# One layer of a hybrid streaming encoder on one core: x and the first part of w_ada arrive laid out by feature block, and the first three projection blocks begin with 704 of 1056 tokens

## The chip, the core and the metric

The kernel runs on one core of a Trainium2 chip. A core has five engines, each with its own in-order list of instructions: PE (TensorE, matrix products into PSUM), ACT (ScalarE), DVE (VectorE), POOL (GpSimd) and SP (SyncE, which here only starts transfers). Sixteen DMA engines move data between HBM and the on-chip memory SBUF. An engine waits at an instruction until the semaphores that it names have been raised, and everything behind that instruction on the same engine waits with it.

The metric is the device time of one execution in microseconds (us). Three executions of the kernel before took 1600.66, 1601.08 and 1601.70 us, so the median is 1601.08 us.

## The reference

T = 1056 tokens (1024 of a prompt and 32 of a sample) of D = 1024 features go through one layer. What matters here is its beginning:

```python
mod = jax.nn.silu(c) @ w_ada + b_ada
sh1, sc1, gt1, sh2, sc2, gt2 = jnp.split(mod[:, None, :], 6, axis=-1)

h = rmsnorm(x, g_mix) * (1 + sc1) + sh1
u = h @ w_in
qa, ka, va, qm, km, vm, om, ip, fp, ga, gm = jnp.split(u, _split_points(), axis=-1)
```

Prompt and sample have a condition c of their own, so sh1 and sc1 are two vectors of 1024 each. rmsnorm(x, g) is x * rsqrt(mean(x*x) + 1e-6) * g. Attention over qa, ka, va, an mLSTM, two projections, a second norm and an FFN follow. The first inputs of the layer are w_ada[:, 0:2048] (8 MB, for sh1 and sc1), x (4.3 MB) and the columns of w_in.

## The kernel before

Features lie on the 128 partitions: x, h and all later activations are held as eight feature blocks of 128 x 1056 (KD = 8). The tokens are cut into three tiles of 352 (TILES). A projection block is 128 columns of w_in. For accuracy each float32 operand is split in two fp32r parts, a high one (rounded) and a low one (the rest), and a product is three passes (PASSES): high by high, low weight by high h, high weight by low h. One tile of one block is therefore 8 feature blocks x 3 passes = 24 products of 128x128 by 128x352.

The order on PE, ACT, DVE and POOL is the order in which the code is written; no scheduler changes it. SP's transfers go in the order written as far as buffers are free. The front of the program, up to the first blocks of attention, runs as follows.

- **x.** Eight transfers bring x token by token (L220). DVE sums the squares of each token (square_sum, L273), PE turns the 64 pieces of 128x128 with transposes (L281), and ACT copies them out of PSUM (L282). POOL makes the reciprocal roots (L299, a power of -0.5), and PE and ACT spread them over the partitions as RB (bcast_cols, L242 and L245).
- **w_ada.** Eight transfers of 1 MB bring its rows (L264). For each, PE forms the part of sc1 (first_ada, L322: eight float32 matmuls, two instructions each in the trace) and DVE the part of sh1 (shift_part, L314). The sum for sh1 over the partitions is taken by PE at the end (row_sums, L348 and L352). Since every element of sh1 and sc1 needs all rows of w_ada, no block of h is ready before the last transfer.
- **h.** For feature block j, scaled_x (L375, DVE) multiplies x by scale and RB, high_h (L386, ACT) adds the shift and rounds, low_h (L392, DVE) forms the low part.
- **First products.** first_units(L475) runs the K and V blocks of head pair 0 together, feature block by feature block, over all three token tiles: 144 products. K is accumulated in three banks of the pool mm (three buffers), V in psS and psT. In the last feature block K's products come first, so that ACT takes K out (L553, L556) while PE does V's.
- **Then** unit() (L443) runs the Q block, 72 products, with buffers of mm, and V's transposes (L612) stand between them. The block behind it, K of head pair 1, is the first of the regular run that fills the rest of the front part of the layer. Weights of a block are split by ACT (L409) and DVE or POOL (L410) into four buffers of the pool wsp; the next two halves wait there for the buffers of the block that is done.

x by features is also written to HBM (xres, L1508) and read back for the residual add (L1552). The pool tmp has four buffers of 128 x 1056 float32. The last feature block of the first products is ordered by this line, which the prediction's last wait turns on:

```python
            if k == KD - 1:
                order.sort(key=lambda x: (x[0], x[2]))
```

Of the kernel before, what the change touches and what calls it, by code (L numbers as in the profile page):

```python
# [17 lines left out]
P = 128  # L18
# [121 lines left out]
def hybrid_stream_step(  # L140
    ctx: ExitStack,
    tc: tile.TileContext,
    x_prompt, x_sample, cache_k, cache_v, state_conv, state_C, state_n, state_m,
# [9 lines left out]
    xp, xs_in = x_prompt[0], x_sample[0]  # L153
    w_in, w_ada, w_out, w_down = w_in[0], w_ada[0], w_out[0], w_down[0]
# [53 lines left out]
    ssq = cp.tile([P, NB], F32, name="ssq")  # L208
    pool.memset(ssq, 1.0)
# [4 lines left out]
    xtok = []  # L214

    for i in range(KD):
        if i % 2 == 0:
            xt = slot([P, 2, D])
            xtok += [xt[:, 0], xt[:, 1]]
        sp.dma_start(xtok[i], xp[i * P:(i + 1) * P])  # L220
    pool.dma_start(cols, params)
    xsm = tmpt((TS, D))
    sp.dma_start(xsm, xs_in)


    csil = cp.tile([P, KD, 2], F32, name="csil")

    def param_cols():
        act.activation(csil, cols[:, R_C:R_C + 16].rearrange("p (c k) -> p k c", c=2), AF.Silu)
# [19 lines left out]
    rstd = cp.tile([P, NB], F32, name="rstd")  # L249
    xres = dr.tile([KD, P, T], F32, name="xres")  # L250
    xTs, xTp, xns = [], [], []
    for j in range(KD):
        if j % 2 == 0:
            xT2 = slot([P, 2, T])
            xTp.append(xT2)
        xTs.append(xT2[:, j % 2])

    was = []
    first_ws, first_cols = [], (KA, VA)

    def load_ada(n):
        while len(was) < n:
            wa = slot([P, 2048])
            sp.dma_start(wa, w_ada[len(was) * P:(len(was) + 1) * P, 0:2048])  # L264
            was.append(wa)

    load_ada(KD)

    def square_sum(i):
        n = P if i < 8 else TS  # L270
        src = xtok[i] if i < 8 else xsm
        junk = tmpt((P, D), BF16)
        dve.tensor_tensor_reduce(junk[:n], src, src, 1.0, 0.0, ALU.mult, ALU.add, ssq[:n, i:i + 1])  # L273

    def x_transposes(g, j):

        pt = mmt()
        for n in range(2):
            for i in range(2):
                at = (2 * n + i) * P  # L280
                pe.transpose(pt[:, at:at + P], xtok[2 * g + i][:, (j + n) * P:(j + n + 1) * P], ident)  # L281
        act.activation(xTp[j // 2][:, :, g * 256:(g + 1) * 256], pt.rearrange("p (n t) -> p n t", n=2), AF.Copy)  # L282

    for g in range(4):
        for i in range(2):
            square_sum(2 * g + i)
# [1995 lines left out]
```

## Time and profile before

| What | Value |
|---|---|
| median of three executions | 1601.08 us |
| the profiled execution, its own time | 1600.87 us |
| its span in the trace | 1598.5 us |
| granted PE clock in that execution | 0.998 |
| DVE busy in the span | 70% |
| ACT busy in the span | 50% |
| POOL busy in the span | 26% |
| last of the eight blocks of x (L281 goes on) | 14.45 us |
| last of the eight blocks of w_ada (L322 goes on) | 36.22 us |

All times in the trace count from the start of the span; the execution's own time is 2.4 us longer than the span. A row of the timeline gives start, length, engine, source line, instruction, what it writes and reads, the number of instructions merged into it, and in brackets how long the engine had been idle before it and what it had waited for. A row of the groups gives the line, the shape, the count, then busy us and mean ns of one instruction, then the idle time before them.

### The profile page before, as it was taken

Reading aid. Unit: us, or ns where it says so; the run is one execution under the profiler, and the core shown is the slowest. Engines: PE = TensorE matmul, PEld = TensorE weight load, DVE = VectorE, ACT = ScalarE, POOL = GpSimd, SP = SyncE. Lnnn points to the kernel's source line nnn. Section 1 sums busy time; section 2 is a strip of 40 time slices with the busy share of each in tenths; the row PEclk is TensorE's granted clock in tenths of the full one; section 3 lists DMA queues with packets and bytes.
Section 4 is the critical chain, followed back from the end, with each engine's and each line's share of the span. In section 5 each row is a group of like instructions: output and inputs, shape, how many; then the busy total and the mean of one; then the engine's idle time right before and its main releaser. Section 6 shows DMA issues by size and latency. Waiting matters only on the chain.

```text
span 1598.5 us, 27336 instructions
## 1 busy us (share of the span) xinstructions
PE 1569.2 (98%) x10197; PEld 1549.3 (97%) x10197; DVE 1122.9 (70%) x2285; ACT 791.3 (50%) x1749; POOL 423.3 (26%) x450
## 2 busy tenths in 40 slices
PE   7999999999999999999999999999999999999997
PEld 6999999999999999999999999999999999999997
DVE  7766555556766845546655699898898986799754
ACT  3665463544555545444434655544445444544443
POOL 1343242433223311000012100675565650000001
PEclk9999999999999999999999999999999999999999
DMA  9823223343132332775453311223222237427454
GB/s 362 268 81 97 94 83 108 91 137 109 36 97 65 87 86 87 127 257 174 130 152 113 96 55 59 89 67 105 70 88 86 68 94 240 136 80 251 137 153 127
DMA packets 209906, 193.48 MB, mean 121 GB/s; under 512 B 11483, under 2 KB 179071, under 8 KB 208751
## 3 DMA queue, kind: packets, MB, share of 16 engines
q1 hardware_dynamic: 207214, 189.92, 38.7%
q10 hardware_dynamic: 2528, 1.77, 0.4%
q8 instruction: 80, 1.31, 0.4%
q14 instruction: 52, 0.42, 0.1%
q0 software_dynamic: 32, 0.06, 0.0%
HBM read 153.24 MB, written 41.63 MB: 122 GB/s over the span
## 4 chain that ended last, share of the span: by engine, by line
PE 91%; DVE 3%; DMA 2%; ACT 2%; issue 1%; SPq 0%; POOL 0%; ACTq 0%; DVEq 0%; POOLq 0%
PE mm L443 41%; PE psb L1811 18%; PE mm L1811 10%; PE mm L2214 3%; PE mm L878 3%; PE psb L2214 2%; PE psV L783 2%; PE psb L2057 2%; PE psS L725 2%; DMA s<-in_w_ada_dram 1%; PE psT L752 1%; PE mm L2057 1%; DMA t<-in_x_sample_dram 1%; PE psV L1112 1%; PE mm L475 1%
## 5 line engine op out<-in xcount | busy, mean ns | idle before, releaser
L443 PE MATMUL mm<-s,wsp 128*128 128x352 f32 x4104 | 687.0, 324 | 0.1
L443 PEld LDWEIGHTS mm<-s,wsp 128*128 128x128 f32 x4104 | 657.3, 188 | 1.8 <-issue 0.4
L410 DVE TENSOR_TENSOR wsp<-wraw,wsp 128x512 fp32r<-128x512 f32 (+1 forms) x280 | 235.6, 858 | 127.4 <-ACT wsp L409 125.3
L1811 PE MATMUL psb<-s,wsp 128*128 128x352 f32 x1611 | 271.7, 322 | 1.6 <-DVE wsp L410 0.9
L409 ACT ACTIVATE wsp<-wraw 128x512 fp32r<-128x512 f32 x336 | 199.5, 617 | 139.0 <-PE psb L1811 42.4
L1811 PEld LDWEIGHTS psb<-s,wsp 128*128 128x128 f32 x1611 | 260.5, 188 | 2.1 <-DVE wsp L410 1.1
L1811 PE MATMUL mm<-s,wsp 128*128 128x352 f32 x933 | 159.3, 322 | 0.0
L1811 PEld LDWEIGHTS mm<-s,wsp 128*128 128x128 f32 x933 | 151.2, 188 | 0.5 <-DVE wsp L410 0.5
L745 POOL TENSOR_SCALAR st<-st,mx 128x640 f32<-128x640 f32 (+5 forms) x72 | 53.1, 738 | 186.3 <-DVE mx L744 168.3
L1207 DVE CUSTOM_DVE_ANT_0 junk<-wa,t 128x512 bf16<-128x512 f32 x128 | 94.9, 742 | 2.8 <-DMA wa<-in_w_mod_dram 1.8
L410 POOL TENSOR_TENSOR wsp<-wraw,wsp 128x512 fp32r<-128x512 f32 x56 | 74.1, 1343 | 58.2 <-ACT wsp L409 56.8
L739 DVE CUSTOM_DVE_ANT_0 st<-psS,bias 128x640 f32<-128x640 f32 (+5 forms) x72 | 44.5, 618 | 57.1 <-PE psS L725 41.9
L740 ACT ACTIVATE st<-st,mx 128x640 f32<-128x640 f32 (+5 forms) x72 | 47.9, 666 | 63.2 <-DVE mx L739 62.1
L1758 POOL TENSOR_TENSOR t<-t,sl 128x352 f32<-128x352 f32 x19 | 18.4, 968 | 213.1 <-ACT sl L1756 213.1
L759 ACT ACTIVATE pT<-psT 128x640 fp32r<-128x640 f32 (+3 forms) x80 | 38.7, 493 | 62.6 <-PE psT L752 47.5
L2126 POOL TENSOR_TENSOR fst<-fst 128x1 f32<-128x1 f32 (+1 forms) x6 | 1.2, 192 | 236.7 <-ACT t L2119 236.7
L764 DVE TENSOR_TENSOR pT<-psT,pT 128x640 fp32r<-128x640 f32 (+3 forms) x80 | 44.0, 558 | 22.2 <-ACT pT L759 22.2
L1420 POOL TENSOR_TENSOR wraw<-wraw,raw 128x512 f32<-128x512 f32 x33 | 55.8, 1704 | 0.9
L878 PE MATMUL mm<-s,s 128*128 128x264 f32 (+3 forms) x432 | 54.5, 283 | 0.0
L2214 PE MATMUL mm<-s,wsp 128*128 128x352 f32 x330 | 54.4, 324 | 0.0
L2214 PEld LDWEIGHTS mm<-s,wsp 128*128 128x128 f32 x330 | 53.0, 188 | 0.0
L878 PEld LDWEIGHTS mm<-s,s 128*128 128x128 f32 (+1 forms) x432 | 52.0, 179 | 0.5
(369 smaller groups left out, 2482.2 us busy)
## 6 DMA issues: line engine op xcount, KB each, us to landing
wraw<-in_w_in_dram SPq DMA_DIRECT2D x38, 512.0 KB, 4.0
wraw<-in_w_gate_up_dram SPq DMA_DIRECT2D x33, 512.0 KB, 3.9
wa<-in_w_mod_dram SPq DMA_DIRECT2D x64, 256.0 KB, 2.8
wraw<-in_w_down_dram SPq DMA_DIRECT2D x32, 512.0 KB, 4.1
a_d<-t SPq DMA_DIRECT2D x22, 528.0 KB, 2.7
g_d<-t SPq DMA_DIRECT2D x16, 528.0 KB, 3.7
x<-xres SPq DMA_DIRECT2D x16, 528.0 KB, 8.6
t<-g_d SPq DMA_DIRECT2D x16, 528.0 KB, 4.5
```

The source lines that it names most:

```text
L409: act.activation(dst[:, 0], src, AF.Copy)
L410: eng.tensor_tensor(dst[:, 1], src, f(dst[:, 0]), op=ALU.subtract)
L443: pe.matmul(pt[:, :hi - lo], wt[(w0 + k) // 4][:, a, (w0 + k) % 4], xt[k][:, b, lo:hi], start=(k == 0 and q == 0), stop=(k == n - 1 and q ...
L739: dve.tensor_tensor_reduce(so, sv, bi, -1.0, 3.0e38, ALU.add, ALU.min, mx[:n, 1:2])
L740: act.activation(st[:n, :w], st[:n, :w], AF.Exp, bias=mx[:n, 1:2], scale=-1.0, accum_out=mx[:n, 2:3])
L745: pool.tensor_scalar(st[:n, :w], st[:n, :w], mx[:n, 3:4], 1.0, op0=ALU.mult, op1=ALU.mult)
L878: pe.matmul(pt[:n, :wd], hs[k][:, a, i * P:i * P + n], whl[b][:, k, :wd], start=(k == 0 and q == 0), stop=(k == KD - 1 and q == 2))
L1207: dve.tensor_tensor_reduce(junk, wa, crow[:, c], 1.0, 0.0, ALU.mult, ALU.add, at)
L1420: self.eng.tensor_tensor(a(dst), a(x), a(y), op=op)
L1811: pe.matmul(acc, wt[:, a, k], x[k][:, b], start=(start and not onto and k == 0 and q == 0), stop=(stop and k == 3 and q == 2), skip_group_ ...
L2057: pe.matmul(acc, wt[k // 4][:, u, k % 4], piece_of[k, i][:, v], start=(k == 0 and q == 0), stop=(k == KP - 1 and q == 2))
L2214: pe.matmul(acc, wt[(k - k0) // 4][:, u, (k - k0) % 4], piece_of[k, 2][:, v], start=(k == 0 and q == 0), stop=(k == NF - 1 and q == 2))
```

## The change

**Inputs.** x comes transposed from the host, one array of eight feature blocks (128 x 1056). The first 2048 columns of w_ada come as two sets of eight tiles of 128 x 1024, one tile for each feature block of sc1 ("scale") and one for each of sh1 ("shift"), so that one tile of 512 KB holds all that a feature block of the output needs. The shift tiles of blocks 0 to 2 are stored with the input features on the partitions, like the scale tiles; those of blocks 3 to 7 with the output features on the partitions.

**Order of the transfers.** First tokens 0 to 703 of the eight blocks of x (CUT = 704, eight transfers of 352 KB), then w_ada's tiles of block 0, the first halves of the K, V and Q weights, w_ada's tiles of block 1, the last 352 tokens of x, w_ada's tiles of block 2, the second weight halves, and the tiles of blocks 3 to 7. The small array of parameters (cols) is started by ACT instead of POOL.

**Conditioning.** PE and ACT make a copy of silu(c) on all partitions (crow), by 16 transposes and four activations. sc1 of a block is eight float32 matmuls with two moving columns (scale_sums, L324). sh1 of blocks 0 to 2 is made in the same way, and of blocks 3 to 7 by DVE, one reduction for each condition (shift_sums, L331).

**Squares.** ACT squares x (L296), DVE adds two blocks at a time (L299), PE sums over the partitions with a column of ones (token_sums, L309). This is done for the 704 early tokens first, and for the 352 late ones in rounds 1 and 2 of the products.

**Rounds.** first_units now runs K, V and Q of head pair 0 on the two early token tiles: in round k the 18 products of feature block k stand in three groups of six (one for each pass), with the scale sums of block k+1 between the first and the second group, and in rounds 1, 2 and 3 the sums of the late squares, and the spreading of the late roots, between the second and the third. Behind the eight rounds come 48 products of K and V on the late tile; Q's late tile is left to unit(). h is made in place: scaled_x multiplies x by RB (DVE), high_h and whole_h (both ACT, with scale and shift) give the rounded and the whole h, and low_h (DVE) the difference.

The x transposes, square_sum, first_ada, row_sums, and the first write of x to xres are gone; the residual add reads x from the input.

The diff, cut to its core:

```diff
-    for i in range(KD):
...
-        sp.dma_start(xtok[i], xp[i * P:(i + 1) * P])
-    pool.dma_start(cols, params)
+    act.dma_start(cols, params)
...
+    CUT = TILES[2][0]
     for j in range(KD):
...
+        sp.dma_start(xTs[j][:, :CUT], x_t[j][:, :CUT])
+
+    first_cols = (KA, VA, QA)
...
+    crow = slot([P, 2, D])
+    load_ada()
+    load_first(0)
+    load_ada()
+    for i, xp in enumerate(xTp):
+        sp.dma_start(xp[:, :, CUT:], x_t[2 * i:2 * i + 2].rearrange("n p t -> p n t")[:, :, CUT:])
+    load_ada()
+    load_first(1)
+    for _ in range(3, KD):
+        load_ada()
...
+    SHIFT_PE = 3
...
+    def conditioning():
...
+        for c in range(2):
+            for h in range(2):
+                pt = mmt()
+                for i in range(4):
+                    k = R_C + 8 * c + 4 * h + i
+                    pe.transpose(pt[:, i * P:(i + 1) * P], cols[:, k:k + 1].to_broadcast([P, P]), ident)
+                act.activation(crow[:, c, h * 512:(h + 1) * 512], pt, AF.Silu)
...
+    def square(j, lo, hi):
+        sq[j] = tmpt()
+        act.activation(sq[j][:, :hi - lo], xTs[j][:, lo:hi], AF.Square)
...
+    def token_sums(j, tiles, begin, end):
...
+                pe.matmul(tok[:b - a, col:col + 1], sq[j][:, a - a0:b - a0], ones[:, 0:1],
+                          start=(begin and col == 0), stop=end, skip_group_check=True)
...
+    def scale_sums(j, i=0):
+
+        at = 2 * (KD * i + j)
+        for k in range(KD):
+            pe.matmul(psH[:, at:at + 2], was[j][:, i, k * P:(k + 1) * P], csil[:, k], start=(k == 0), stop=(k == KD - 1),
+                      skip_group_check=True)
...
+    def shift_sums(j, c):
+        dve.tensor_tensor_reduce(junk, was[j][:, 1], crow[:, c], 1.0, 0.0, ALU.mult, ALU.add, sha[:, c, j:j + 1])
...
+    def scaled_x(j, lo, hi):
+        x = xTs[j][:, lo:hi]
+        dve.tensor_tensor(x, x, RB[:, lo:hi], op=ALU.mult)
...
+            act.activation(hs[j][:, 0, a:b], xTs[j][:, a:b], AF.Identity, scale=s1[:, c, j:j + 1],
+                           bias=sh1[:, c, j:j + 1])
+
+    def whole_h(j, lo, hi):
...
+            act.activation(x, x, AF.Identity, scale=s1[:, c, j:j + 1], bias=sh1[:, c, j:j + 1])
+
+    def low_h(j, lo, hi):
+        dve.tensor_tensor(hs[j][:, 1, lo:hi], xTs[j][:, lo:hi], f(hs[j][:, 0, lo:hi]), op=ALU.subtract)
...
+        pts = [[S[:, :512], S[:, 512:]], [psA[:, :512], mmt()], [mmt(), mmt()], ]
+        last = [tok, psH]
...
+        def late_squares(j0, j1):
+            for j in range(j0, j1):
+                square(j, *late)
+                if j > j0:
+                    add_squares(j0, j, NT)
+            token_sums(j0, [late], j0 == 0, j1 == KD)
...
+        for k in range(KD):
+            n = k + 1
+            for i in range(3):
+                for t in range(2):
+                    product(k, i, 0, t)
+            if n < KD:
+                scale_sums(n)
+                if n < SHIFT_PE:
+                    scale_sums(n, 1)
+                else:
+                    shift_sums(n, 0)
+                scaled_x(n, 0, CUT)
+                scale_done(n)
+                shift_done(n, 0)
+                high_h(n, 0, CUT)
+                whole_h(n, 0, CUT)
+            low_h(k, 0, CUT)
+            for i in range(3):
+                for t in range(2):
+                    product(k, i, 1, t)
             if k in (1, 2):
-                if k == 1:
-                    first_split(1)
+                late_squares(4 * k - 4, 4 * k)
+            if k == 3:
+                token_roots(2, 0)
...
+            if SHIFT_PE <= n < KD:
+                shift_sums(n, 1)
+                shift_done(n, 1)
+            late_h(k - 3)
+            for i in range(3):
+                for t in range(2):
+                    product(k, i, 2, t)
...
+        for k in range(KD - 3, KD + 2):
+            late_h(k)
+        for k in range(KD):
+            for q in range(3):
+                for i in range(2):
+                    product(k, i, q, 2)
...
+        W.advance()
...
-            yield lo, hi, done[t] if done else unit(w, 0, hs, lo, hi)
+            yield lo, hi, done[t] if done and t < len(done) else unit(w, 0, hs, lo, hi)
...
-    for j in range(KD):
-        sp.dma_start(xres[j], xTs[j])
-    first_units([run.w for run in segs[0][1][:2]])
+    first_units()
...
-        sp.dma_start(x2[j], xres[j])
+        sp.dma_start(x2[j], x_t[j])
```

Three places in the order of the instructions matter. The number behind a name is that of its buffer. First PE, where the products begin. Before, the last sums for sh1 stand ahead of the first products of K (mm_61, mm_62) and V (psS_60, psT_47) and between them; in the seven rounds behind this piece there are products alone:

```order
L352 MATMUL psV_46_266<-csil_107,s_17_128 128x64
L348 MATMUL psV_46_266<-ones_85,t_49_269 128x64
L352 MATMUL psV_46_266<-csil_107,s_17_128 128x64
L348 MATMUL psT_47_267<-ones_85,t_48_268 128x64
L475 MATMUL mm_61_426<-s_65_432,wsp_56_398 128x352
L475 MATMUL psS_60_425<-s_65_432,wsp_58_400 128x352
L348 MATMUL psT_47_267<-ones_85,t_48_268 128x64
L475 MATMUL mm_62_427<-s_65_432,wsp_56_398 128x352
L475 MATMUL psS_60_425<-s_65_432,wsp_58_400 128x352
L348 MATMUL psT_47_267<-ones_85,t_48_268 128x64
L475 MATMUL mm_63_428<-s_65_432,wsp_56_398 128x352
L475 MATMUL psT_47_267<-s_65_432,wsp_58_400 128x352
```

After, this is the middle of round 1 (h block s_45), from the last product of the first pass over the scale and shift sums of block 2 (16 float32 matmuls into psV), the second pass, and the sums of the late squares (t_47) to the first product of the third pass:

```order
L453 MATMUL mm_40_285<-s_45_325,s_44_294 128x352
L324 MATMUL psV_20_152<-csil_93,s_11_124 128x2 x16
L453 MATMUL psS_37_282<-s_45_325,wsp_33_261 128x352 x2
L453 MATMUL psT_19_151<-s_45_325,wsp_42_289 128x352
L453 MATMUL mm_38_283<-s_45_325,wsp_42_289 128x352
L453 MATMUL mm_39_284<-s_45_325,s_44_294 128x352
L453 MATMUL mm_40_285<-s_45_325,s_44_294 128x352
L309 MATMUL psT_19_151<-ones_85,t_47_376 128x1 x2
L309 MATMUL psT_19_151<-ones_85,t_47_376 96x1
L453 MATMUL psS_37_282<-s_45_325,wsp_33_261 128x352 x2
```

The small matmuls moved from ahead of the products into the rounds, and the third pass of round 1 now stands behind the late squares on PE.

Second, ACT in the same rounds. Before, one round on ACT is the rounding of one block of h and the 32 sample tokens apart (here two rounds):

```order
L386 ACTIVATE s_71_568<-s_70_545,sh1_270 128x1024
L385 ACTIVATE s_70_545<-s_70_545,sh1_270 128x32
L386 ACTIVATE s_71_568<-s_70_545 128x32
L386 ACTIVATE s_72_594<-s_70_545,sh1_270 128x1024
L385 ACTIVATE s_70_545<-s_70_545,sh1_270 128x32
L386 ACTIVATE s_72_594<-s_70_545 128x32
```

After, ACT takes sc1 and sh1 out of PSUM (s1, sh1), makes the high and the whole h of blocks 1 and 2 (s_45, s_46), and then squares the late tokens of blocks 0 to 3 (t_47 to t_50):

```order
L328 ACTIVATE s1_150<-psV_20_152,gb1_147,cols_91 128x2
L337 ACTIVATE sh1_149<-psV_20_152,cols_91 128x2
L351 ACTIVATE s_45_325<-s_1_95,sh1_149,s1_150 128x704
L357 ACTIVATE s_1_95<-s_1_95,sh1_149,s1_150 128x704
L328 ACTIVATE s1_150<-psV_20_152,gb1_147,cols_91 128x2
L337 ACTIVATE sh1_149<-psV_20_152,cols_91 128x2
L351 ACTIVATE s_46_366<-s_2_96,sh1_149,s1_150 128x704
L357 ACTIVATE s_2_96<-s_2_96,sh1_149,s1_150 128x704
L296 ACTIVATE t_47_376<-s_1_95 128x352
L296 ACTIVATE t_48_378<-s_1_95 128x352
L296 ACTIVATE t_49_381<-s_2_96 128x352
L296 ACTIVATE t_50_384<-s_2_96 128x352
```

The squares for which PE's row t_47 waits come behind the whole h of block 2, and that behind the scale and shift sums of block 2 on PE.

Third, the end of the first products on ACT. Before, ACT takes the K block (mm_61 and on) out of PSUM and only then splits the next weights (wsp_82, wsp_83):

```order
L386 ACTIVATE s_79_658<-s_73_598 128x32
L553 ACTIVATE s_80_682<-mm_61_426 64x352 x2
L553 ACTIVATE s_80_682<-mm_62_427 64x352 x2
L556 ACTIVATE kf_81_683<-mm_62_427 128x192
L553 ACTIVATE s_80_682<-mm_63_428 64x352 x2
L556 ACTIVATE kf_81_683<-mm_63_428 128x352
L409 ACTIVATE wsp_82_698<-wraw_75_629 128x512
L409 ACTIVATE wsp_83_699<-wraw_75_629 128x512
L587 ACTIVATE t_85_708<-psS_60_425 128x352 x2
L587 ACTIVATE t_85_708<-psT_47_267 128x352
```

After, the split of the next weights (wsp_63, wsp_64, in the buffers of the K weights) stands ahead, and then K's tiles (psS_37, psT_19) and V's (psT_19, mm_38):

```order
L368 ACTIVATE wsp_63_724<-wraw_59_579 128x512
L368 ACTIVATE wsp_64_725<-wraw_59_579 128x512
L566 ACTIVATE s_66_732<-psS_37_282 64x352 x4
L569 ACTIVATE kf_67_733<-psS_37_282 128x192
L566 ACTIVATE s_66_732<-psT_19_151 64x352 x2
L569 ACTIVATE kf_67_733<-psT_19_151 128x352
L600 ACTIVATE t_68_750<-psT_19_151 128x352
L600 ACTIVATE t_68_750<-mm_38_283 128x352
L600 ACTIVATE t_68_750<-psV_20_152 128x352
L652 ACTIVATE t_71_759<-mm_39_284 128x352
```

On PE the last of the late products and the first of Q's late tile then stand thus; that tile's bank, mm_74, is the third buffer of mm again, which V's second tile (mm_38) holds until ACT has read it:

```order
L453 MATMUL psT_19_151<-s_62_603,wsp_34_262 128x352
L453 MATMUL psV_20_152<-s_62_603,wsp_43_290 128x352
L453 MATMUL psT_19_151<-s_62_603,wsp_34_262 128x352
L453 MATMUL psV_20_152<-s_62_603,wsp_43_290 128x352
L402 MATMUL mm_74_779<-s_41_287,s_44_294 128x352 x3
L402 MATMUL mm_74_779<-s_45_325,s_44_294 128x352 x3
```

The first product of Q's late tile moved behind ten instructions of ACT, the second of which, the split into wsp_64, waits for the last product that reads the K weights.

305 lines of the change are left out of this document (118 added, 187 removed).

## The prediction

> **What bounds the kernel now.** The page first, its busy times by engine:
>
> ```profile
> PE 1569.2 (98%) x10197; PEld 1549.3 (97%) x10197; DVE 1122.9 (70%) x2285; ACT 791.3 (50%) x1749; POOL 423.3 (26%) x450
> ```
>
> PE is the bound: a change of the front is worth what it moves the moment from which PE runs its regular blocks. Two rows of the timeline fix the front: the first product, and the first product of the block behind Q, K of head pair 1.
>
> ```profile
> 41.34 0.43 PE L475 MATMUL mm<-s,wsp 128*128 128x352 f32 x1 [0.65 <-ACT s L386]
> 81.52 5.94 PE L443 MATMUL mm<-s,wsp 128*128 128x352 f32 x36
> ```
>
> So PE reaches the regular run at about 81.4 us. How much of that is waiting? The busy times by stage, cut at the first data, the first product and that moment, and then PE's two longest waits up to there:
>
> ```profile
> 0.00:4.64 4.64, 0.00 (x0) 0.03 (x1) 0.00 (x0) 1.28 (x1) 1.63 (x10) 1.00 0.54 189
> 4.64:41.33 36.69, 30.63 (x231) 27.61 (x231) 30.79 (x41) 13.56 (x33) 2.52 (x2) 1.00 1.01 379
> 41.33:81.36 40.03, 39.31 (x247) 37.93 (x248) 31.15 (x46) 24.93 (x54) 14.28 (x17) 1.00 0.82 271
> ...
> PE mm L281 <- DMA s<-in_x_prompt_dram: 6.6, 3, 4.6
> PE psT L322 <- DMA s<-in_w_ada_dram: 3.0, 6, 0.7
> ```
>
> The first busy column is PE's, the last two numbers are the share of the DMA engines and GB/s. From 4.64 to 41.33 PE idles 6.1 us, mostly for transfers, and from there to 81.36 only 0.7. The front looks bound by DMA (share 1.01), and the chain of waits runs through w_ada; yet PE has 70 us of its own work in it. An earlier start helps only so far: waiting less can gain 7 us at most, unless PE's work shrinks.
>
> **The change part by part.** Does it shrink? Prices on PE: a stretch of 18 products, x's transposes, eight of L322's matmuls (two instructions each), and float32 matmuls with one moving column, which stand elsewhere in the program:
>
> ```profile
> 90.72 2.88 PE mm L443 x18
> ...
> 5.83 2.39 PE L281 MATMUL mm<-ident,s 128*128 128x128 f32 x10 [0.74 <-DMA s<-in_x_prompt_dram]
> ...
> 7.59 5.67 PE L281 MATMUL mm<-ident,s 128*128 128x128 f32 x40
> ...
> 17.26 2.05 PE L322 MATMUL psT<-csil,s 128*128 128x128 f32 x16
> ...
> 894.93 0.36 PE L1583 MATMUL psV<-ones,sl 128*128 128x1 f32 x2
> 895.15 0.36 PE L1581 MATMUL psV<-ones,t 128*128 128x1 f32 x2
> 895.38 0.36 PE L1583 MATMUL psV<-ones,sl 128*128 128x1 f32 x2
> 895.60 0.31 PE L1581 MATMUL psV<-ones,t 128*96 128x1 f32 x2
> 895.77 0.31 PE L1583 MATMUL psV<-ones,sl 128*96 128x1 f32 x2
> ```
>
> A product takes 2.88/18 = 0.16 us, a transpose 5.67/40 = 0.14. A float32 matmul with one moving column starts 0.225 us after the one before (two steps from 894.93 to 895.38), hardly less than L322's 2.05/8 = 0.256 with 128; with only 96 weight columns it is 0.17. Two-column matmuls are not in the trace, so I take 0.225, the nearest row, and keep 0.17 and 0.256 as ends. After, PE has 88 of them for scale and shift (3x16 + 5x8) and 30 for token sums, 26.6 us. They replace 64 of L322 (16.4), 22 row sums at about 0.225 (5.0) and 72 transposes of x (10). With crow's 16 transposes (2.3 to 3.8) the new work is 29 to 30 us against 31. PE's work does not shrink; what is left to win is the idle time.
>
> Prices of ACT, DVE and POOL, from the groups by shape (mean ns behind the busy time), and nine copies in a row:
>
> ```profile
> L1610 ACT ACTIVATE s<-x,amod 128x352 fp32r<-128x352 f32 x16 | 9.3, 588 | 7.9 <-DVE x L1609 7.9
> L1627 ACT ACTIVATE x<-x,amod 128x32 f32<-128x32 f32 x8 | 2.5, 311 | 0.0
> L1027 ACT ACTIVATE s<-t,cols 128x1024 f32<-128x1024 f32 x8 | 9.9, 1234 | 0.0
> L409 ACT ACTIVATE s<-x 128x352 fp32r<-128x352 f32 x68 | 29.4, 484 | 0.0
> L409 ACT ACTIVATE s<-s 128x1056 fp32r<-128x1056 f32 x4 | 4.3, 1082 | 2.2 <-DVE s L1241 2.2
> 9.32 4.53 ACT L282 ACTIVATE s<-mm 128x512 f32<-128x512 f32 x9 [0.26 <-PE mm L281]
> L1561 DVE TENSOR_TENSOR t<-t,t 128x352 f32<-128x352 f32 x24 | 12.6, 526 | 0.8
> L1241 DVE TENSOR_TENSOR s<-s,s 128x1056 f32<-128x1056 f32 x4 | 5.0, 1260 | 2.6 <-ACT s L1240 2.6
> L273 DVE CUSTOM_DVE_ANT_0 t<-s 128x1024 bf16<-128x1024 f32 x8 | 9.7, 1225 | 6.0 <-DMA s<-in_x_prompt_dram 5.8
> L1588 POOL TENSOR_TENSOR rs<-rs,mhalf 128x4 f32<-128x4 f32 x3 | 3.3, 1086 | 19.5 <-DVE rs L1586 19.5
> ```
>
> On the lines between these, 704 columns cost ACT 0.93 with scale and shift and 0.78 without (a square), and DVE 0.89; a tiny activation costs 0.28, a shift reduction 1.3 with its read-out, a power 1.1. Independent copies start about 0.1 before the one before has ended (nine of 0.6 in 4.53).
>
> *Up to the first product.* It needs crow's place on ACT, the squares of 704 tokens, and RB. The start of the timeline, and the transfer of cols:
>
> ```profile
> cols<-in_params_dram POOLq DMA_DIRECT2D x1, 62.0 KB, 5.9
> ...
> 0.82 3.89 SPq L220 DMA_DIRECT2D s<-in_x_prompt_dram  x8
> ...
> 6.76 0.60 ACT L282 ACTIVATE s<-mm 128x512 f32<-128x512 f32 x1 [4.67 <-PE mm L281]
> 7.62 0.60 ACT L282 ACTIVATE s<-mm 128x512 f32<-128x512 f32 x1 [0.26 <-PE mm L281]
> ...
> 25.00:30.00 5.00, 4.11 (x35) 3.73 (x34) 4.97 (x5) 0.00 (x0) 0.00 (x0) 1.00 1.02 423
> ```
>
> Cols took 5.9 us to land. Started by ACT among x's first transfers it should land with x's first block, which PE had at 4.64; I take 4.6, between 3.5 (it is only 62 KB) and 7.5 (as slow as before). Four transposes and a copy came every 0.86 us (6.76 to 7.62), so crow, four of these, is done at 8.8. ACT, in order, then squares eight blocks, 0.7 each back to back and half a us lost to the adds: 15.3. DVE's last add ends at 16.2, PE's last six sums at 17.6; then PE has 16 matmuls for block 0 (3.6 us, under which the two powers, 2.2, are hidden; were they not, they would cost that much), the transposes of the roots, and then come RB, s1 and sh1, and the high h: first product at 23.7 instead of 41.3. Data is there: at 0.42 MB per us the 4.7 MB of early x, block 0 and three weight halves land by about 16, all 14.3 MB by about 40, and w_ada's last tiles are wanted after 70. SP issues 34 transfers here instead of 21, at 0.49 us (3.89/8) half the time that they take to move. Gain **17.6**.
>
> *Behind it.* 216 products are 34.6 us in both. The small matmuls of blocks 1 to 7 (72) and of the late squares (6) now stand here, 17.6, and three transposes, 0.4; before, 11 row sums did, 2.5. V's nine transposes, 1.4, stand ahead of the moment 81.4 now and behind Q's last tile after, so that they come on top there. Loss 18.0 + 1.4 - (2.5 + 1.4) = **15.5**.
>
> *New waits.* Round 1: once PE has done the sums of block 2, ACT needs s1 and sh1 (0.6), the high and the whole h (1.85), four squares (1.6, and 0.4 waiting for an add), DVE the last add (0.5): with handovers 5.2, of which PE's second pass covers 1.0. The token sums, and behind them on PE the third pass, wait 4.2. Round 2 is the same with 1.4 for the adds, since two buffers of tmp are all that is left to the squares: 5.3. Round 3: the late roots cross DVE, POOL, PE and ACT, 1.4. Block 0's second tile, 0.9. Rounds 4 and 6 wait for DVE, which has two reductions and 704 and 352 columns twice, 5.2 a round back to back, against PE's 18 x 0.16 + 8 x 0.225 = 4.7: together 2.1. Last, Q's late tile waits for the bank of V's second tile. ACT's copies out of PSUM at this place now, K's and V's:
>
> ```profile
> 66.65 1.88 ACT L553 ACTIVATE s<-mm 64x352 fp32r<-64x352 f32 x4 [3.55 <-PE mm L475]
> 68.54 0.33 ACT L556 ACTIVATE kf<-mm 128x192 f32<-128x192 f32 x1
> 69.69 0.46 ACT L556 ACTIVATE kf<-mm 128x352 f32<-128x352 f32 x1
> 71.96 0.80 ACT L587 ACTIVATE t<-psS 128x352 f32<-128x352 f32 x2
> ```
>
> They run beside PE's products of V and Q. After, ACT starts the split into wsp_64 only when K's last product is done (0.6), then takes out six half tiles of K (6 x 0.47), kf (0.8) and two tiles of V (0.9), some 5.2 in all, with PE idle. Sum of the waits 19.1, against 81.4 - 41.3 - 34.6 - 2.5 - 1.4 = 1.6 now: loss **17.5**.
>
> Sum: 23.7 + 34.6 + 18.0 + 1.4 + 19.1 = 96.8 instead of 81.4, **15.4 us later**. What lies behind is PE's own work and moves as a whole. The first writes of x to xres gain nothing by their absence: ACT and POOL waited for them once, PE never.
>
> **Rivals.** (1) The late squares do not hold PE (adds and squares get done earlier than I reckon): 4.2 + 5.3 less, so +5.9 and 1606.8. For it speaks that ACT is only half busy; against it that each group crosses ACT, DVE and PE in a fixed order behind the sums of the next block.
>
> (2) PE's clock falls in the new gaps. After its first 4.6 us without work PE made ten transposes in 2.39 us, 0.24 each, and later forty at 0.14: 1.0 us lost. After three gaps over 4 us as much each is +3, 1619.3. The granted clock reads 1.00 throughout, so the trace leaves open whether the clock was the cause. [...]
>
> (3) The other side: behind the first product PE waits for nothing, because ACT and DVE keep ahead of it. Then 96.8 - 19.1 = 77.7, 3.7 earlier than 81.4: 1597.2. It decides as soon as the waits sum to less than 3.7; the last one alone is 5.2.
>
> (4) The change does not bring what it says: the early start is eaten exactly, 1600.9.
>
> **How the numbers follow.** The profiled execution took 1600.87 us, 0.2 under the median of 1601.08. 1600.9 + 15.4 = 1616.3; I say 1616. My forecast has a chance of 0.64, with its own ends from cols (-1.1 to +2.9), the small matmuls (118 at 0.17 to 0.256: -6.5 to +3.7, the low end only if two columns are far cheaper than one) and ACT's tiny instructions (1.5 either way): 1609 to 1622. Rival 1 has 0.14, rival 2 0.11, rival 3 0.05, rival 4 0.06. The range takes in rivals 1 and 2: 1606 to 1623. Faster by over 0.2% (3.2 us, about what a measurement of this kernel can tell from no change) has 0.05, the same 0.06, slower 0.89.
>
> **What would show it.** Right: a first product near 24 us, three idle times of PE of 4 to 5 us (before L309 in rounds 1 and 2, before the first L402), and K of head pair 1 near 95. Wrong: L324 under 0.17 us a matmul, or L309 without a wait, towards rivals 1 and 3; products at twice their time behind a gap would be rival 2. A gap of PE that comes from a transfer would upset the whole sum.

## The result, and the profile after

The changed kernel takes 1648.23 us (median of 4 runs, 1642.10 to 1649.23), the kernel before 1601.39 (4 runs): a ratio of 1.0282, 95% interval 1.0270 to 1.0294. It is slower, as forecast, but by 47 us instead of 15. The profiled span grew from 1598.5 to 1646.1, by 47.6.

The page of the changed kernel, its busy times by engine and PE's clock in 40 slices of 41 us:

```profile
PE 1600.2 (97%) x10205; PEld 1580.4 (96%) x10205; DVE 1108.3 (67%) x2287; ACT 813.1 (49%) x1786; POOL 416.0 (25%) x440
...
PEclk9689999999999999999999999999999999999999
```

PE executes 8 instructions more than before and is busy 31 us longer. That cannot be waiting; and slices two and three say that the clock was at 0.6 and 0.8. Before, all 40 digits are 9. The stages, cut at the first product and at the first product of the block behind Q (the columns are those of the prediction's windows):

```profile
0.00:30.49 30.49, 21.27 (x103) 20.58 (x103) 5.74 (x12) 12.12 (x21) 2.53 (x11) 1.00 0.98 346
30.49:123.67 93.18, 76.80 (x375) 73.85 (x376) 43.85 (x74) 47.89 (x100) 8.01 (x9) 0.74 0.36 123
```

The first product came 10.9 us earlier (41.34 to 30.49), forecast 17.6. From there to K of head pair 1 it took 93.2 us instead of 40.2 (81.52 - 41.34), 53.0 more, forecast 31.6. Behind that another 5.4 were lost (47.6 + 10.85 - 53.0), forecast 1.4. PE's longest waits up to there:

```profile
PE psT L309 <- DVE t L299: 11.4, 3, 5.1
PE mm L402 <- ACT t L600: 6.3, 1, 6.3
PE mm L288 <- DMA cols<-in_params_dram: 4.5, 1, 4.5
PE psS L453 <- ACT s L351: 2.1, 2, 1.7
```

The long waits are those of the forecast, at its places. Behind the first product the waits sum to 16.4 us (93.18 - 76.80), forecast 19.1. So the loss is in PE's *busy* time: 76.8 us where the forecast had 34.6 of products and 18.0 of small matmuls. The timeline of PE (start, length, line, operation, count, in brackets the idle time before) shows how:

```profile
11.20 9.52 PE L309 MATMUL psT<-ones,t 128*128 128x1 f32 x48 [3.06 <-DVE t L299]
20.58 6.97 PE L324 MATMUL psV<-csil,s 128*128 128x2 f32 x32
27.41 1.41 PE L227 MATMUL mm<-ident,roots 128*128 128x128 f32 x6
30.49 0.66 PE L453 MATMUL psS<-s,wsp 128*128 128x352 f32 x1 [1.66 <-ACT s L351]
...
40.63 0.49 PE L453 MATMUL psT<-s,wsp 128*128 128x352 f32 x1
40.92 0.49 PE L453 MATMUL mm<-s,wsp 128*128 128x352 f32 x1
...
43.66 0.32 PE L453 MATMUL psT<-s,wsp 128*128 128x352 f32 x1
43.82 0.33 PE L453 MATMUL mm<-s,wsp 128*128 128x352 f32 x1
...
69.56 0.49 PE L453 MATMUL psT<-s,wsp 128*128 128x352 f32 x1
69.85 0.49 PE L453 MATMUL mm<-s,wsp 128*128 128x352 f32 x1
...
95.85 1.84 PE L324 MATMUL psV<-csil,s 128*128 128x2 f32 x16
...
118.22 5.61 PE L402 MATMUL mm<-s,s 128*128 128x352 f32 x24 [6.33 <-ACT t L600]
123.67 1.61 PE L402 MATMUL mm<-s,wsp 128*128 128x352 f32 x9
```

A product follows the one before after 0.29 us at 40.63, 0.16 at 43.66, and 0.29 again at 69.56. A small matmul (two instructions) takes 6.97/16 = 0.44 us at 20.58 and 1.84/8 = 0.23 at 95.85. These are two speeds of PE, a factor of 1.8 to 1.9 apart, and the slow one holds for most of the front. The first two rows join without a break: from 11.20 to 27.40 PE is busy in all of the 16.2 us, and it stays slow. By windows of the changed kernel (clock in the third column from the right):

```profile
30.00:45.00 15.00, 14.08 (x64) 13.71 (x64) 5.17 (x7) 5.37 (x9) 0.00 (x0) 1.00 0.86 339
45.00:61.00 16.00, 12.77 (x64) 12.31 (x64) 4.93 (x8) 4.62 (x9) 0.00 (x0) 0.57 0.48 164
...
65.00:90.00 25.00, 22.01 (x85) 21.19 (x86) 16.14 (x28) 9.33 (x19) 0.85 (x1) 0.50 0.18 53
```

From 65 to 90 the granted clock is 0.50 while the DMA engines are busy for a share of only 0.18, so contention with DMA is hardly the cause. In the first row the clock reads 1.00 although products of 0.29 stand in it: the column reads 1.00 up to the clock's first fall, here at 46.5 us by windows of 0.25 us, and does not show the slow stretch before that. The steps between products do. By the same fine windows the clock then is down from 46.5 to 60.1, from 63.5 to 90.8 and from 114.7 to 121.6.

### The profile page after: what moved, and what is told of

It reads as the page before. It is cut to its first block, busy times and chain, and to the rows that moved or that the text cites. A ratio compares the mean times of both kernels' runs of the same rounds, so it can differ in the third digit from the quotient of the medians.

```text
span 1646.1 us, 27360 instructions
## 1 busy us (share of the span) xinstructions
PE 1600.2 (97%) x10205; PEld 1580.4 (96%) x10205; DVE 1108.3 (67%) x2287; ACT 813.1 (49%) x1786; POOL 416.0 (25%) x440
## 4 chain that ended last, share of the span: by engine, by line
PE 88%; issue 4%; ACT 4%; DVE 3%; POOL 0%; DMA 0%; ACTq 0%; DVEq 0%; POOLq 0%
PE mm L402 39%; PE psb L1813 18%; PE mm L1813 10%; PE mm L2216 3%; PE mm L890 3%; PE psb L2216 2%; PE psV L795 2%; PE psb L2059 2%; PE psS L736 1%; PE psT L763 1%; PE mm L2059 1%; PE psT L309 1%; PE psV L1124 1%; PE psT L1126 1%; PE psT L1121 1%
```

## The experiments

That PE runs at half clock in the front is in the trace (0.50 from 65 to 90 us). *Why* it does isn't, and two theories compete.

- **Theory 1, narrow matmuls**: matmuls with one or two moving columns count as no work for the clock. A stretch of them neither raises it nor holds it, though PE is never idle in it; gaps lower it too.
- **Theory 2, gaps**: only PE's idle times lower the clock; the small matmuls are innocent.

For the length of a slow stretch behind a wait, the changed kernel's trace shows 5.8 us behind the first long one (54.35 to 60.1), 23 behind the second (67.63 to 90.8) and 3.4 behind the last (118.22 to 121.6).

The first four runs cross the two causes. Lines of the runs are shifted by a few against the changed kernel: the products stand at L455 or L463 in some.

### Wide matmuls, the gaps kept

```
 scale_sums:
-  pe.matmul(psH[:, at:at + 2], was[j][:, i, k * P:(k + 1) * P], csil[:, k], ...)
+  pe.matmul(psH[:, at:at + P].rearrange("p (r c) -> p r c", c=2), was[j][:, i, k * P:(k + 1) * P],
+            csil[:, k].unsqueeze(1).to_broadcast([P, DH, 2]), ...)
 token_sums:
-  pe.matmul(tok[:b - a, col:col + 1], sq[j][:, a - a0:b - a0], ones[:, 0:1], ...)
+  pe.matmul(tok[:b - a, col * DH:col * DH + DH], sq[j][:, a - a0:b - a0], ones[:, 0:1].to_broadcast([P, DH]), ...)
 ...                    # the columns of PSUM that are read move with them
```

> The changed kernel, in which the small matmuls of the front get more moving columns with the same values: the sums for scale and shift 128 instead of 2, the token sums 64 instead of 1. Their number, their order and every wait stay. Theory 1 (narrow matmuls): a stretch of matmuls with one or two moving columns counts as no work for PE's clock, so that it neither rises nor holds, though PE is never idle in it; then the wide ones bring full speed by about 18 us, the first product comes near 26 instead of 30.5, products take 0.16 us except for some 3 to 7 us behind each of the three long waits, and the time is about 1634 (1628 to 1640). Theory 2 (gaps): only PE's idle times hold the clock down; they are all still there, so products behind them still take 0.29, and the wider matmuls cost 2 to 3 us: 1648 to 1652.

Measured: 1634.68 us (ratio 1.0207, 1.0191 to 1.0222), 13.6 below the changed kernel, at the middle of theory 1. More work for each matmul made the kernel faster. PE's timeline in this run:

```profile
11.04 9.43 PE L309 MATMUL psT<-ones,t 128*128 128x64 f32 x48 [3.06 <-DVE t L299]
20.26 6.01 PE L324 MATMUL psV<-csil,s 128*128 128x128 f32 x32
...
30.62 3.73 PE L324 MATMUL psV<-csil,s 128*128 128x128 f32 x32
...
46.02 1.44 PE L309 MATMUL psT<-ones,t 128*128 128x64 f32 x6 [4.23 <-DVE t L299]
47.21 0.93 PE L455 MATMUL psS<-s,wsp 128*128 128x352 f32 x2
```

The scale sums with 128 columns reached full speed: 3.73/16 = 0.233 us at 30.62. The first product stood at 28.59, between the 30.49 of the changed kernel and the 26 expected. The token sums with 64 columns did *not* raise the clock in 9.4 us (9.43/24 = 0.39 each), which neither theory had foreseen. Behind the wait of 4.23 us PE is slow again (6 instructions in 1.44, against 0.72 at full speed in a later run): the clock fell at 45.4, inside the wait, so gaps do lower it too.

### Narrow matmuls, the gaps gone

```
-  pts = [[S[:, :512], S[:, 512:]], [psA[:, :512], mmt()], [mmt(), mmt()], ]
+  pts = [[mmt(), mmt()], [psA[:, :512], S[:, :512]], [mmt(), S[:, 512:]]]
 ...
   if k == 3:
       token_roots(2, 0)
+  if k in (2, 3):      # ahead of late_squares, which no longer calls token_sums
+      token_sums(4 * k - 8, [late], k == 2, k == 3)
 ...                    # the late roots' transposes and RB go to k == 4, late_h(0) with them
-  W.advance()          # at the end of first_units
```

> The changed kernel without its three long waits, the small matmuls as narrow as they were: the late token sums stand a round behind their squares, the late roots and what follows them half a round to a round later, K's two early tiles lie in the banks that Q's late tile and the next block want first, and the split for the next weights comes behind K's evictions. Theory 1 (narrow matmuls): the waits of 3.2, 5.1 and 6.3 us go, and Q's late tile runs at full speed, but the rounds before the fifth or sixth still run at 0.29 us a product: about 1632 (1626 to 1638). Theory 2 (gaps): behind the first product there is no gap to lower the clock, products take 0.16 from round 1 on, and another 20 us go: about 1612 (1606 to 1618).

Measured: 1626.65 us (1.0162, 1.0145 to 1.0179), 21.6 below the changed kernel. Its rows of PE:

```profile
39.80 0.93 PE L453 MATMUL mm<-s,wsp 128*128 128x352 f32 x2
...
44.72 4.28 PE L324 MATMUL psV<-csil,s 128*128 128x2 f32 x32
48.86 0.93 PE L453 MATMUL mm<-s,wsp 128*128 128x352 f32 x2
...
56.01 0.57 PE L453 MATMUL mm<-s,wsp 128*128 128x352 f32 x2
...
67.03 0.95 PE L453 MATMUL mm<-s,wsp 128*128 128x352 f32 x2 [2.44 <-DVE s L360]
```

Two products take 0.93 at half speed and 0.57 at full. The clock came up and fell again, at 47.5, inside the 16 small matmuls (32 instructions) from 44.72. It came back at 54.3 and fell twice more, at 57.7 and 64.6, both times at the end of a group of three token sums. From 31.6 to 64.5 PE was busy in all of the 32.9 us, so none of the three falls has a gap ahead of it: this is what theory 2 excludes, and it missed by 15 us. Theory 1 lies at its lower edge; that the clock was up for stretches from 54.3 on, earlier than I expected, fits this. A new wait for the low h, 2.44 us at 67.03, shows that the rearrangement did not remove all gaps.

### Both edits

> Both edits of the two runs before together: wide small matmuls and no long waits. Theory 1 (narrow matmuls) and the cooling by gaps both gone: first product near 26, full speed from about 18 us on, the block behind Q begins near 87: about 1606 (1600 to 1612), the lowest of the four. Theory 2 (gaps): no better than without the wide matmuls, 2 to 3 us above it.

Measured: 1619.68 us (1.0113, 1.0098 to 1.0128): the lowest of the four, but 13.7 above what theory 1 expected, and 7 *below* the run without the wide matmuls, where theory 2 wanted it above. The four medians:

| | gaps kept | gaps gone |
|---|---|---|
| 1 and 2 columns | 1648.23 | 1626.65 |
| 64 and 128 columns | 1634.68 | 1619.68 |

Wide matmuls are worth 13.6 or 7.0 us, the gaps 21.6 or 15.0. Of these, 11.7 and 12.2 us are the waiting itself: from the first product to K of head pair 1 PE idles 16.4 us in the changed kernel and 4.7 without the gaps, and with wide matmuls 19.4 and 7.2. The savings do not add up, which fits that either cause brings the clock down where the other would. This run's own profile says where the rest is:

```profile
11.02 9.62 PE L309 MATMUL psT<-ones,t 128*128 128x64 f32 x48 [3.06 <-DVE t L299]
...
27.83 0.43 PE L455 MATMUL mm<-s,wsp 128*128 128x352 f32 x1 [1.71 <-ACT s L353]
...
47.17 0.72 PE L309 MATMUL psT<-ones,t 128*128 128x64 f32 x6
50.25 0.82 PE L455 MATMUL mm<-s,wsp 128*128 128x352 f32 x2 [2.35 <-DVE s L362]
```

The opening is slow again (9.62/24 = 0.40 us a token sum), and the first product stood at 27.83 instead of the forecast's 23.7. Behind a wait of 2.35 us for DVE the clock fell again (at 50.4); three matmuls of 64 columns stand ahead of it. Behind the waits of 1.71 and 0.67 us around the first product it fell without any (at 30.0), but behind the same 1.71 and 0.67 us in the run with the gaps kept it did not (1.00 from 25 to 35), and why is not shown.

### The kernel before with narrow matmuls

The opposite edit, in a kernel whose front has no long gap:

```
-  out = psA[:, b * P:(b + 1) * P]
-  c = csil[:, k].unsqueeze(1).to_broadcast([P, DH, 2])
-  pe.matmul(out.rearrange("p (r c) -> p r c", c=2), was[k][:, D + b * P:D + (b + 1) * P], c, ...)
+  pe.matmul(psA[:, b * P:b * P + 2], was[k][:, D + b * P:D + (b + 1) * P], csil[:, k], ...)
```

> The kernel before with one edit: its 64 scale matmuls, which have 128 moving columns with two values alternating, get only the two. Each becomes shorter, nothing else changes, and no gap of PE in that stretch is over 1.2 us. Theory 1 (narrow matmuls): the clock falls within the stretch from 17 to 38 us; the row sums and the first products behind it run at half speed for 3 to 7 us: 2 to 5 us slower than before, 1603 to 1606. Theory 2 (gaps): no change, 1601, products at 0.16 from the first.

Measured: 1612.06 us (1.0065, 1.0050 to 1.0080), 11.4 slower, for 64 matmuls that each have 126 columns less. Its timeline of PE, and its windows:

```profile
17.87 1.95 PE L320 MATMUL psT<-csil,s 128*128 128x2 f32 x16
19.67 1.24 PE L242 MATMUL mm<-ident,rstd 128*128 128x128 f32 x9
20.84 24.05 PE L320 MATMUL psT<-csil,s 128*128 128x2 f32 x112
```

```profile
15.00:20.00 5.00, 4.29 (x39) 3.79 (x38) 3.40 (x7) 3.65 (x14) 2.04 (x2) 1.00 1.01 419
20.00:25.00 5.00, 5.00 (x28) 4.79 (x26) 4.85 (x4) 1.18 (x3) 0.00 (x0) 0.58 1.01 415
25.00:30.00 5.00, 5.00 (x25) 5.00 (x25) 3.85 (x4) 0.00 (x0) 0.00 (x0) 0.50 1.01 419
```

This settles it. The first 16 instructions run at full speed, 0.24 us a matmul. Then 112 stand in one unbroken row, at 24.05/56 = 0.43 us each. By fine windows the clock falls at 20.85, just as this row begins; PE had then been busy without a break since 16.53, for 4.3 us, behind a wait of 0.70. The kernel before waits 1.19 us near the same place (ahead of 14.45), and its clock never falls. So no idle time is there to blame, and 24 us in which PE is never idle do not bring the clock back. Theory 2 is wrong as the whole cause. Theory 1 was right in kind and too small in size (2 to 5 us): I had priced the products behind, and forgotten that the narrow matmuls themselves then take 0.43 instead of 0.256, so that they outlast w_ada's transfers, which had hidden them.

### Where is the limit?

Three more widths in the same 64 matmuls of the kernel before, and a run with 128 columns in the first 16 and 64 in the other 48:

> The kernel before with 64 moving columns instead of 128 in its 64 scale matmuls: where does the clock's need lie? With two columns this stretch took 0.427 us a matmul and PE reached K of head pair 1 at 90.9, with 128 at 81.5. If half the columns count as enough work, the clock stays up, a matmul takes about 0.225 and the time is 1601 or a little less. If not, the clock falls as with two columns, a matmul takes about 0.43 and the time is 1610 to 1613.

> The same with 32 moving columns. If the need lies under a quarter of 128 columns, 1601; if it lies above, as with two columns: 0.43 us a matmul and 1610 to 1613. If 64 columns already let the clock fall, this must too.

> The kernel before with 96 moving columns instead of 128 in its 64 scale matmuls. With 64 and with 32 the clock was down in this stretch (0.42 us a matmul, 1611), with 128 it is up (0.256 us, 1601). If what counts is a share of busy array near that of 128, the time is 1608 to 1612; if a little over half is enough, 1600 to 1602 with 0.24 us a matmul.

> The kernel before with 128 moving columns in the scale matmuls of the first two blocks of w_ada and 64 in the other six: the clock is up when the narrower ones begin. If 64 columns hold a raised clock and only fail to raise it, 0.225 us a matmul to the end and 1601; if they count as too little work either way, the clock falls some 3 to 7 us into them, with no gap, and the time is 1606 to 1611.

With 2 columns the clock had fallen 3.0 us after the first of them (17.87 to 20.85), with 32 some 6.7 us after (17.95 to 24.6, from the clock of 0.96 in the window from 20 to 25).

| columns | median us | us a matmul |
|---|---|---|
| 2 | 1612.06 | 0.24, then 0.43 |
| 32 | 1610.68 | 0.235, then 0.43 |
| 64 | 1611.93 | 0.43 to 0.45 from the start |
| 128, then 64 | 1609.57 | 0.25, then 0.43 |
| 96 | 1601.44 | 0.253 |
| 128 (before) | 1601.4 | 0.256 |

The run with 96 is equal to the kernel before (1.0000, 0.9989 to 1.0011), and its clock never falls. One of its rows, and a window:

```profile
25.74 2.02 PE L322 MATMUL psT<-csil,s 128*128 128x96 f32 x16 [0.31 <-DMA s<-in_w_ada_dram]
```

```profile
25.00:30.00 5.00, 4.21 (x36) 3.88 (x35) 5.00 (x5) 0.00 (x0) 0.00 (x0) 1.00 1.01 421
```

The run with 64 from the first on shows only that they do not raise a clock that is down: it fell there at 18.5, 0.2 us after their first and behind a wait of 1.35 us, and stayed at 0.50 through 29 us of them without a gap. The run that begins with 128 decides whether 64 columns hold a raised clock:

```profile
20.70 2.05 PE L323 MATMUL psT<-csil,s 128*128 128x128 f32 x16
23.63 2.00 PE L323 MATMUL psT<-csil,s 128*128 128x64 f32 x16 [0.87 <-DMA s<-in_w_ada_dram]
26.12 17.13 PE L323 MATMUL psT<-csil,s 128*128 128x64 f32 x80 [0.49 <-DMA s<-in_w_ada_dram]
```

```profile
25.00:30.00 5.00, 4.51 (x25) 4.37 (x25) 4.97 (x5) 0.00 (x0) 0.00 (x0) 0.64 1.02 424
```

At full clock, eight matmuls take 2.00 us with 64 columns, 2.02 with 96 and 2.05 with 128. Yet behind them the 64 columns go at half speed, 17.13/40 = 0.43: the clock fell at 26.4, 2.7 us after their first. The waits beside them, 0.87 and 0.49 us, are about as long as those of the kernel before at this place (0.67 and 0.44), which with 128 columns lower nothing. So in these runs 64 columns neither raised the clock (0.50 through 29 us) nor held it (0.50 from 26.4 on), and 96 held it (1.00 throughout); the limit for these float32 matmuls with 128 x 128 weights lies between. Whether 96 would also raise it, no run shows.

### A mended kernel

The edit in short:

```
+  warm(12); conditioning(); warm(12)       # 24 transposes of the identity, result unused
   early token sums and scale sums with 128 moving columns
   late squares and adds, and the late whole_h:  act / dve  ->  pool
   token_sums(0, [late], tok, DH, True, True) once, at k == 2
   banks and W.advance() as in the run without gaps
```

> The changed kernel mended at all places that the runs so far name: scale, shift and early token sums with 128 moving columns; 12 transposes of the identity before crow's and 12 behind them, whose result nobody reads, to bring the clock up; the late squares and their adds, and the late tile's whole h, on POOL, one set of late token sums in round 2; K's early tiles in the banks that are wanted first and the split behind K's evictions. Theory 1 (narrow matmuls and gaps): full speed from about 10 us, first product at 24 to 25, no wait over 1.5 us behind it, K of head pair 1 near 82, and 4 to 6 us more behind that than before: 1605 (1600 to 1609). Theory 2 (gaps alone): the same. If POOL slows DVE or ACT by working beside them, waits come back before low h: 1610 and more.

Measured: 1608.30 us (1.0041, 1.0026 to 1.0055), inside the expectation, 40 below the changed kernel and still 6.7 above the kernel before. K of head pair 1 comes at 84.42, not near 82. The three stages of its profile:

```profile
0.00:23.32 23.32, 17.71 (x126) 16.45 (x126) 5.98 (x11) 12.00 (x21) 4.42 (x14) 1.00 0.96 336
23.32:84.42 61.10, 56.82 (x369) 54.57 (x370) 44.20 (x66) 36.49 (x72) 34.32 (x33) 0.94 0.54 189
84.42:110.00 25.58, 22.30 (x140) 20.68 (x138) 14.83 (x38) 18.63 (x40) 12.98 (x18) 1.00 0.52 160
```

With the clock up, the first product stands at 23.32, where the forecast had it: the chain from cols to the first h was counted right. From there to K of head pair 1 it takes 61.1 us instead of 40.2. Of these 20.9 us, 3.6 are more waiting (4.3 against 0.7). Some 3 are the clock, which by fine windows was down from 24.1 to 27.5 and from 51.4 to 54.9, with 6.5 us of busy time in it. The other 14 or so are work that the change moved behind the first product. The early start brings 18.0, so the moved work alone would not eat it; the waits, the clock and 5.2 us lost behind that block do. Both falls stand in the second of a pair of short waits, 2.12 and 0.67 us, then 1.29 and 1.01, with no narrow matmul near them.

A last run moved the shift sums of blocks 1 and 2 to DVE:

```
-    SHIFT_PE = 3
+    SHIFT_PE = 1       # and the host's layout of w_ada's shift for blocks 1 and 2
```

> The run before with the shift sums of blocks 1 and 2 on DVE instead of PE (and their weights laid out for that): 16 matmuls of 0.256 us fewer on PE, 4.1 us, four reductions of 1.22 us more on DVE. If DVE has that room in rounds 0 and 1, where it idled 5 us at a time: 4 us below the run before, 1601 (1597 to 1605). If not, its reductions hold the scaled x and PE waits for it: no better than the run before.

Measured: 1609.96 us (1.0055, 1.0040 to 1.0070), no better. The wait on which PE loses most in this run shows where the saving went:

```profile
PE mm L463 <- DVE s L368: 7.0, 6, 2.2
```

PE waits six times for the low h on DVE, 7.0 us in all against 1.9 in the run before, 5.1 more, against the 4.1 us of matmuls saved. No version of the change tried here beats the kernel before.

## Why the prediction was wrong

**Which step failed.** The direction was right, and all the waits named came but those for DVE. The step that failed is the price of the small matmuls, "I take 0.225, the nearest row": it took a few steps at full clock (from 894.93) as the price of 118 such matmuls, most of them in long rows. At full clock the price is right (1.84/8 = 0.23 at 95.85). Sixteen in a row brought the clock down here (at 46.5, in the row from 44.30) and in the run without gaps (at 47.5), for themselves and for the products behind them, and a clock that was down they left down. The range left this out: its ends, 0.17 and 0.256, were both prices at full clock. Term by term, in us:

| term | forecast | measured | missed |
|---|---|---|---|
| first product earlier | -17.6 | -10.9 | 6.7 |
| waits behind it | 19.1 | 16.4 | -2.7 |
| products and small matmuls to K of head pair 1 | 52.6 | 76.8 | 24.2 |
| behind K of head pair 1 | 1.4 | 5.4 | 4.0 |

The misses sum to 32.2, which is 47.6 - 15.4. The clock is large enough for the third row: between the first product and K of head pair 1 PE was busy at the slow speed for 48.8 us (12.3 of them up to 43.25, the rest in the three stretches named above). At the factor of 1.8 to 1.9, this is an estimated 22 to 23 us lost, of 24.2.

**First product.** Cols landed as reckoned (PE starts at 4.50, taken 4.6). The token sums then ended at 20.7 instead of 17.6, and the 16 matmuls of block 0 took 6.97 us instead of 3.6. In the mended kernel, with wide matmuls and the clock up, the token sums ended at 17.0, the 16 matmuls took 3.73 and the first product stood at 23.32: the chain was right, and the term was mis-sized by the clock.

**Waits.** Rounds 1 and 2: 3.2 and 5.1 us, forecast 4.2 and 5.3. The bank at the end: 6.3, forecast 5.2. Round 3: 0.4 instead of 1.4; block 0's second tile: 0.4 instead of 0.9. These are the mechanisms named, with sizes within 1.1. For DVE in rounds 4 and 6 PE waited not at all instead of 2.1: round 4 ran at half speed, which gave DVE time, but round 6 ran at full speed and did not wait either, and why is not shown. Two waits of 0.5 for the late low h were not in the forecast.

**The rivals.** Rival 2 ("PE's clock falls in the new gaps") was the right kind of event with the wrong condition and price. I took three gaps at 1.0 us each from the ten slow transposes before. But the gaps cost more: nearly half of all busy time until the clock was up again (0.29 us a product instead of 0.16). From 67.63 to 90.8 the trace is slow for 23 us, in which eight small matmuls (3.4 us) alternate with 5.2 us of products. With 128 columns in the small matmuls the clock was up some 6.3 us behind the same wait (from 59.61 to about 65.9 in the run with the gaps kept; it reads 0.91 from 65 to 70). Rivals 1 and 3 rested on waits that would not come; they came.

In a row of products the clock rose: in the changed kernel a product took 0.29 us from 39.9 on and 0.16 from 43.3. In a row of narrow matmuls it did not: 16 us of them without a gap (11.20 to 27.40) left PE at half speed, 0.44 us each from 20.58 on, and in the run without gaps the clock fell three times (at 47.5, 57.7 and 64.6) while PE was never idle. Nor did a gap have to be over 4 us: in the mended kernel 2.12 and 0.67 us close together were enough. So it was not enough here that PE was busy.

**Behind K of head pair 1.** "What lies behind is PE's own work and moves as a whole" was wrong by 4.0. The same 40 us of both kernels, from that block on, before first (its two other windows have PE busy in all of 10 us, and a clock of 1.00):

```profile
81.50:91.50 10.00, 9.38 (x60) 9.10 (x59) 8.85 (x17) 6.26 (x13) 5.62 (x9) 1.00 0.54 165
...
101.50:111.50 10.00, 7.98 (x54) 7.46 (x53) 4.49 (x13) 6.45 (x12) 1.60 (x2) 1.00 0.18 50
```

```profile
123.70:133.70 10.00, 9.79 (x65) 9.40 (x65) 4.16 (x10) 7.17 (x14) 4.23 (x6) 1.00 0.34 97
133.70:143.70 10.00, 7.69 (x47) 7.05 (x46) 6.23 (x18) 5.58 (x15) 1.57 (x4) 1.00 0.01 2
143.70:153.70 10.00, 7.57 (x46) 6.80 (x45) 5.72 (x16) 8.04 (x14) 3.92 (x4) 0.93 0.29 81
153.70:163.70 10.00, 10.00 (x64) 9.87 (x63) 5.04 (x13) 4.56 (x10) 1.59 (x2) 0.90 0.04 6
```

PE idles 2.6 us there before and 5.0 after. The attention of head pair 0 begins in both with small steps that wait for ACT and DVE; I take it that its side work, which used to lie beside Q's 72 products, now has too little beside it. And behind these waits the clock falls once more: 0.93 and 0.90 of 10 us each mean 3.4 us at half speed, 1.7 lost. With V's transposes (1.4) that is 2.3 + 1.7 + 1.4 = 5.4. This was read from the rows, not tested by a run; the mended kernel loses 5.2 behind that block too (8.1 more span, + 18.0 - 20.9), with its clock at 1.00, so the split isn't the same in every run.

**Open.** The changed kernel's runs spread over 7 us (1642.10 to 1649.23), those before over 1.7. That the clock rises a round earlier in one run than in another could explain it, but no second trace shows it, and the mean granted clock of the fastest run, 0.977, is the lowest of the four (the others 0.982 and 0.983). In all these runs each small matmul has its own 128 x 128 weights and follows the one before after much the same time at full clock (0.23 to 0.26 us with 128 weight columns), so they do not tell whether the clock goes by the number of columns or by the share of that time in which columns move. Whether the limit between 64 and 96 holds for other types or sizes of weights was not tried, nor how much waiting lowers the clock.

## What to carry to other kernels

Price small matmuls by the clock that they leave behind, not only by their own time: a stretch of them that runs in 0.23 us each at full clock ran in 0.43, and took the products beside it from 0.16 to 0.29. Give them enough moving columns (96 cost the same 2.0 us for eight as 64 did, and held the clock) or spread them between dense work: in the changed kernel eight of them between 18 products left the clock up from 90.8 to 114.7, though the same mix had not raised it for 23 us before. Add up short waits that stand close together: in the mended kernel 2.0 us of idle time between 48.0 and 51.4 lowered the clock. When a change moves small matmuls, look at the step from product to product in each stage before you look at waits.

## What the runs showed of the hardware that was not expected

- It was not enough for the clock that PE was busy; in the 64 scale matmuls of the kernel before their width decided. With 2 and 32 float32 columns on 128 x 128 weights the granted clock went to 0.50 when PE had not been idle for 4.3 and 8.0 us, with 64 beside waits of 0.87 and 0.49 us; with 96 and 128 it stayed at 1.00 beside waits of up to 0.63 and 0.67 us.
- The clock also fell at short waits close together: in the mended kernel it went to 0.50 for some 3.4 us at 2.12 and 0.67 us around one product, and at 1.29 and 1.01. Behind 1.71 and 0.67 us it fell in the run with both edits and not in the run with the gaps kept, and behind 0.29 and 1.73 us some 3 us apart not in the kernel before, so where the limit lies is open.
- At full clock the width changed the time of one of these matmuls little: 0.24 us with 2 columns, 0.25 with 64, 0.253 with 96, 0.256 with 128.
- The column of the granted clock read 1.00 up to the clock's first fall, even where products took 0.29 us each (30 to 45 us of the changed kernel, with the first fall at 46.5).
